# Attention scores over all 128 rows, with the keys of each head laid between zeros

## The chip, the cores and the metric

One core of a Trainium2 chip runs the whole program. The time is the device time of one execution in microseconds. The engines are TensorE (PE; PEld is its weight load), VectorE (DVE), ScalarE (ACT), GpSimd (POOL) and the queue that starts most DMAs (SP).

## The reference

Two layers of a decoder over 256 tokens of width 1024. Each layer has a mixer with two groups of eight heads of 64 columns and then a feed-forward part: a dense SwiGLU in the first layer, the best two of eight experts in the second. Cut to what matters here:

```
u = rmsnorm(h); proj = u @ w_in                       # queries, keys, values of both groups
A: s = q_norm . k_norm * SCALE + bias[dist]           # two key branches (selected, window),
   o = softmax(masked s) @ v                          #   4 query heads share one key head;
                                                      #   and a branch over 15 compressed keys
B: the same with a key and a value head per query head, dilated masks
h = h + [rmsnorm(o_a), rmsnorm(o_b)] @ w_out          # then the feed-forward part
```

With 256 tokens the top-k selection of blocks covers every block, so both branches of group A are dense causal attention.

## The kernel before

All products are matrix products over blocks of 128 tokens (t = 0, 1), with the projections in a two-part form: `product3` (L406) multiplies high and low parts of both operands in three matmuls, L408, L409 and L410. The projection (tile `pj`, L418), the output product (tile `y`, L754) and the scores of group A use it. The weights come in pieces of 1 MB through SP (L74) and are split into their parts by ScalarE (L92) and VectorE (L93).

`attention` first projects group A's keys and values, then its queries, and calls `group_a` (L676) while the projections of group B (`B_CHUNKS`) are still to be done. `heads_t` (L496) turns normalised queries and keys with transposes (tile `ht`, L504), so that the 64 columns of a head lie on 64 of the 128 partitions: two heads share a tile, one on the partitions 0 to 63, the other on 64 to 127. For group A the copies from PSUM are `split_psum` (L340: ScalarE L346 writes the high part, VectorE L347 the low), for group B one ScalarE copy (L509). Queries of group A lie in `qta`, keys in `kta`; group B has both in `qktb`.

`branch` (L511) works through units of heads: the `scores` function fills a PSUM bank (tile `sc`), VectorE adds the bias table and takes the row minimum (L523, tile `ns`), ScalarE takes the exponential with its row sum (L525), four transposes turn the unit's 512 columns (tile `pT`, L532), VectorE or ScalarE copies them (tile `pt`, L537 or L535), and a product with the values follows (tile `o`, L544). Group A has four units for t = 0, with 4 x 128 columns, and eight for t = 1, with 2 x 256; group B two and four. In `scores` a slice `p` of 64 partitions is chosen on both operands:

```
p = slice(g * 64, g * 64 + 64)                                   # group A, L701
product3(..., qh[p, qi, c], ql[p, qi, c], kh[p, :, 0:J], kl[p, :, 0:J], True, True)
```

so each of these matmuls contracts over 64 rows of the array. All others of the stage contract over 128; those of the compression (`hid`, `kvc`) write 32 columns of the array.

The instructions of each engine are put in a fixed order when the program is built, by a scheduler that spreads the matmuls of the next projection, and in group B those of the output product of group A, between the steps of `branch`. An engine goes through its order and waits where an operand is not there yet. Tiles with a tag share memory: `qta` has the tag x2, `qktb` x4, and a new tile with a tag waits for the last reader of the old one. PSUM banks with the tag tr (two) serve the scores, the transposes and several others; group B may use the bank cmp too.

Of the kernel before, what the change touches and what calls it, by code (L numbers as in the profile page):

```python
# [10 lines left out]
F32 = mybir.dt.float32  # L11
F32R = mybir.dt.float32r
# [3 lines left out]
AF = mybir.ActivationFunctionType  # L16
# [5 lines left out]
S = 256  # L22
# [119 lines left out]
def trunk_kernel(ctx: ExitStack, tc: tile.TileContext, T: dict, out: bass.AP):  # L142
    nc = tc.nc
    pe, act, dve, pool, sp = nc.tensor, nc.scalar, nc.vector, nc.gpsimd, nc.sync

    const = ctx.enter_context(tc.tile_pool(name="const", bufs=1))
    main = ctx.enter_context(tc.tile_pool(name="main", bufs=1))
# [9 lines left out]
    def tr_bank(name):  # L157
        return bank("tr", TR, name)
# [23 lines left out]
    for l in range(L):  # L182
# [25 lines left out]
        else:  # L208
            seq = [(e, c) for e in range(NE) for c in range(len(MOE_CHUNKS))]
            first = len(specs)  # L210
            for i in range(len(seq) + 1):
                if i < len(seq):
                    e, c = seq[i]
# [126 lines left out]
    def split_psum(hi, lo, src, scale=None):  # L340

        if scale is None:
            act.activation(hi, src, AF.Copy)
            dve.tensor_tensor(out=lo, in0=src, in1=hi.bitcast(F32), op=ALU.subtract)
        else:
            act.activation(hi, src, AF.Copy, scale=scale)  # L346
            dve.scalar_tensor_tensor(out=lo, in0=src, scalar=scale, in1=hi.bitcast(F32),  # L347
                                     op0=ALU.mult, op1=ALU.subtract)
# [57 lines left out]
    def product3(dst, xh, xl, wh, wl, first, last):  # L406

        pe.matmul(dst, xh, wh, start=first, stop=False)  # L408
        pe.matmul(dst, xl, wh, start=False, stop=False)  # L409
        pe.matmul(dst, xh, wl, start=False, stop=last)  # L410
# [10 lines left out]
    def attention(l, apool, hi, lo, following):  # L421
# [21 lines left out]
        pa = main.tile([128, NT, W_A - 512], F32, name="pa", tag="x6")  # L443
        pb = main.tile([128, NT, 1024], F32, name="pb", tag="x5")
# [48 lines left out]
                    dve.tensor_tensor(out=v, in0=v, in1=r[:, t, 2 * i:2 * i + 2].unsqueeze(2)  # L493
                                      .to_broadcast([128, 2, HD]), op=ALU.mult)

        def heads_t(dst, pj, c0, n, scale):  # L496

            for i in range(0, n, 2):
                m = min(2, n - i)
                b = tr_bank("ht")  # L500
                for j in range(m):
                    for t in range(NT):
                        c = c0 + (i + j) * 128
                        pe.transpose(b[:, j * S + t * 128:j * S + (t + 1) * 128], pj[:, t, c:c + 128], ident)  # L504
                if isinstance(dst, tuple):
                    hi, lo = [d[:, i:i + m, :].rearrange("p i t -> p (i t)") for d in dst]
                    split_psum(hi, lo, b[:, :m * S], scale)
                else:
                    act.activation(dst[:, i:i + m, :].rearrange("p i t -> p (i t)"), b[:, :m * S], AF.Copy, scale=scale)  # L509

        def branch(units, t, scores, vpj, tbl, banks):  # L511

# [162 lines left out]

        def group_a(dq):  # L676
            q = main.tile([128, 2, 4, S], F32R, name="qta", tag="x2")
            k = apool.tile([128, 2, 2, S], F32R, name="kta")
            qh, ql, kh, kl = q[:, 0], q[:, 1], k[:, 0], k[:, 1]
            norm_heads(dq, qa, 0, "qa", paired=True)  # L680
            norm_keys()
            heads_t((qh, ql), qa, 0, 4, qg[:, l:l + 1])
            heads_t((kh[:, 0:1], kl[:, 0:1]), pa, 256, 1, hg[:, 3 + l * 3:4 + l * 3])
            heads_t((kh[:, 1:2], kl[:, 1:2]), pa, 512, 1, hg[:, 4 + l * 3:5 + l * 3])
            if COMPRESS_FIRST:
                bd, kct = compress(kv)

            e3 = apool.tile([128, NT, 24], F32, name="e3")
            act.activation(e3, pa[:, :, 768:792], AF.Exp, scale=-1.0)
            dve.tensor_scalar(out=e3, in0=e3, scalar1=1.0, scalar2=None, op0=ALU.add)  # L690
            dve.reciprocal(out=g3.rearrange("p t i b -> p t (i b)"), in_=e3)

            for t in range(NT):
                J = 128 * (t + 1)
                o = [acc_bank(f"o{br}") for br in range(2)]
                den = [apool.tile([128, 8], F32, name=f"den{br}", tag="den", bufs=4) for br in range(2)]

                def scores(b, u):
                    for i in range(0, len(u), 2):
                        g, qi = divmod(u[i][0], 4)  # L700
                        p = slice(g * 64, g * 64 + 64)  # L701
                        c = slice(t * 128, (t + 1) * 128)
                        product3(b[:, i * J:(i + 2) * J].rearrange("p (b j) -> p b j", b=2), qh[p, qi, c], ql[p, qi, c],
                                 kh[p, :, 0:J], kl[p, :, 0:J], True, True)

                n = 2 // (t + 1)
                units = [[(g * 4 + u * n + i, (384, 640)[br] + g * HD, o[br], den[br])
                          for i in range(n) for br in range(2)] for u in range(4 // n) for g in range(2)]
                branch(units, t, scores, pa, ta, BANKS_A)
                for br in range(2):  # L710
                    combine(o[br], den[br], t, br + 1)
            if not COMPRESS_FIRST:
                bd, kct = compress(kv)
            for t in range(NT):
                compressed(t, qh, ql, kct, bd)

        def group_b(ob):
            qkt = main.tile([128, 8, S], F32, name="qktb", tag="x4")
            qt, kt = qkt[:, 0:4], qkt[:, 4:8]
            heads_t(kt, pb, 512, 4, hg[:, 10 + l:11 + l])  # L720
            heads_t(qt, pb, 0, 4, qg[:, 8 + l:9 + l])
            for t in range(NT):
                J = 128 * (t + 1)
                n = 4 // (t + 1)
                o = acc_bank("o")
                den = apool.tile([128, 8], F32, name="den", tag="den", bufs=4)

                def scores(b, u):
                    for i, (hd, _, _, _) in enumerate(u):
                        qi, r = divmod(hd, 2)  # L730
                        p = slice(r * 64, r * 64 + 64)
                        pe.matmul(b[:, i * J:(i + 1) * J], qt[p, qi, t * 128:(t + 1) * 128], kt[p, qi, 0:J],
                                  start=True, stop=True)

                units = [[(2 * (u * n + i) + r, (2 * (u * n + i) + r) * HD, o, den) for i in range(n)]
                         for u in range(4 // n) for r in range(2)]
                branch(units, t, scores, vb, (tb[:, 0:4], tb[:, 4:8]), BANKS_B)
                rd = apool.tile([128, 8], F32, name="rd", tag="rd", bufs=2)
                dve.reciprocal(out=rd, in_=den)
                dve.tensor_tensor(out=ob[:, t, :].rearrange("p (i d) -> p i d", d=HD),  # L740
                                  in0=o.rearrange("p (i d) -> p i d", d=HD),
                                  in1=rd.unsqueeze(2).to_broadcast([128, 8, HD]), op=ALU.mult)
# [454 lines left out]
    hi, lo = parts()  # L1197
    for c in range(2):
        lift(R_AN, 0, c * 512, 512, hi, lo)
    hg, qg, relb, w2, wr = late_constants()  # L1200
    for l in range(L):
# [23 lines left out]
        if l % 2 == 0:  # L1225
            hi, lo = ffn(l, *nxt)
# [59 lines left out]
```

## Time and profile before

| | |
|---|---|
| median of three runs | 1484.54 us (1482.44 to 1486.54) |
| profiled execution | 1485.44 us, its span 1483.3 us |
| TensorE busy | 1444.2 us, 97% |
| VectorE busy | 1188.5 us, 80% |
| ScalarE busy | 982.4 us, 66% |
| group A, first and second layer | about 56 to 114 us and 400 to 458 us of the span |
| group B, first and second layer | about 136 to 161 us and 479 to 506 us |
| feed-forward of the second layer | from about 540 us to the end |

The stages overlap, since projections and output products run between the steps of the attention; the limits in the table are those between which most of a stage's own instructions lie. In the rows further down a line on busy time gives, behind a stretch and its length, the busy us of PE, PEld, DVE, ACT and POOL, each with its number of instructions in brackets. A timeline line gives start, duration, engine, line, operation, tiles, and in square brackets the idle time before it with what ended it. A record of TensorE runs from the start of a matmul to its modelled end, and records of matmuls that follow one another overlap.

### The profile page before, as it was taken

Reading aid. Unit: us, or ns where it says so; the run is one execution under the profiler, and the core shown is the slowest. Engines: PE = TensorE matmul, PEld = TensorE weight load, DVE = VectorE, ACT = ScalarE, POOL = GpSimd, SP = SyncE. Lnnn points to the kernel's source line nnn. Section 1 sums busy time; section 2 is a strip of 40 time slices with the busy share of each in tenths; the row PEclk is TensorE's granted clock in tenths of the full one; section 3 lists DMA queues with packets and bytes.
Section 4 is the critical chain, followed back from the end, with each engine's and each line's share of the span. In section 5 each row is a group of like instructions: output and inputs, shape, how many; then the busy total and the mean of one; then the engine's idle time right before and its main releaser. Section 6 shows DMA issues by size and latency. Waiting matters only on the chain.

```text
span 1483.3 us, 19457 instructions
## 1 busy us (share of the span) xinstructions
PE 1444.2 (97%) x7166; PEld 1168.7 (79%) x7166; DVE 1188.5 (80%) x1391; ACT 982.4 (66%) x1005; POOL 7.9 (1%) x17
## 2 busy tenths in 40 slices
PE   7999999999999979999999999999999999999997
PEld 6777888888877868877878878888888888888886
DVE  4566855555667669999999999889999888888885
ACT  5455654444555458887887787678787677667773
POOL 2000000000000000000000000000000000000000
PEclk9999999999999979999999999999999999999999
DMA  8822355556734459999999999999999999999990
GB/s 266 289 83 86 128 187 196 193 192 205 229 115 158 141 200 353 393 392 395 394 393 394 394 393 393 394 385 390 395 394 393 389 360 367 328 341 355 366 354 31
DMA packets 201063, 437.72 MB, mean 295 GB/s; under 512 B 9464, under 2 KB 26096, under 8 KB 200944
## 3 DMA queue, kind: packets, MB, share of 16 engines
q1 hardware_dynamic: 198304, 435.16, 80.7%
q8 instruction: 81, 1.33, 0.4%
q10 hardware_dynamic: 2176, 0.52, 0.2%
q0 software_dynamic: 464, 0.40, 0.1%
q14 instruction: 38, 0.31, 0.1%
HBM read 434.45 MB, written 1.08 MB: 294 GB/s over the span
## 4 chain that ended last, share of the span: by engine, by line
PE 86%; DMA 7%; DVE 3%; ACT 1%; issue 1%; SPq 0%; DVEq 0%; ACTq 0%
DMA raw<-in_exp_w_up_dram 7%; PE eg L408 6%; PE eg L409 6%; PE eg L410 6%; PE ey L409 3%; PE ey L410 3%; PE ey L408 3%; PE eu L410 3%; PE eu L409 3%; PE eu L408 3%; PE pj L410 3%; PE pj L408 3%; PE pj L409 3%; PE ey L977 2%; PE y L410 2%; PE y L409 2%
## 5 line engine op out<-in xcount | busy, mean ns | idle before, releaser
L132 DVE TENSOR_TENSOR wlo<-raw,whi 128x2048 fp32r<-128x2048 f32 x336 | 758.2, 2286 | 57.7 <-PE ey L410 19.0
L125 ACT ACTIVATE whi<-raw 128x2048 fp32r<-128x2048 f32 x336 | 638.8, 1914 | 102.6 <-PE eu L409 26.6
L93 DVE TENSOR_TENSOR wlo<-raw,whi 128x1024 fp32r<-128x1024 f32 (+1 forms) x130 | 154.6, 1193 | 103.5 <-ACT whi L92 100.8
L92 ACT ACTIVATE whi<-raw 128x1024 fp32r<-128x1024 f32 (+1 forms) x130 | 133.5, 1032 | 116.7 <-PE y L409 41.3
L408 PE MATMUL eg<-whi,xe 128*128 128x512 f32 x448 | 182.5, 407 | 0.0
L409 PE MATMUL eg<-whi,xe 128*128 128x512 f32 x448 | 177.8, 397 | 0.0
L410 PE MATMUL eg<-wlo,xe 128*128 128x512 f32 x448 | 177.7, 397 | 0.1
L410 PEld LDWEIGHTS eg<-wlo,xe 128*128 128x128 f32 x448 | 84.7, 189 | 20.8 <-DVE wlo L132 0.5
L409 PEld LDWEIGHTS eg<-whi,xe 128*128 128x128 f32 x448 | 84.8, 189 | 17.9
L408 PEld LDWEIGHTS eg<-whi,xe 128*128 128x128 f32 x448 | 84.7, 189 | 17.8
L977 PE MATMUL ey<-wlo,eth 128*128 128x512 f32 x224 | 89.2, 398 | 3.4 <-DVE wlo L132 2.9
L977 PE MATMUL eu<-wlo,xe 128*128 128x512 f32 x224 | 89.0, 397 | 1.9 <-DVE wlo L132 1.8
L410 PE MATMUL eu<-wlo,xe 128*128 128x512 f32 x224 | 88.7, 396 | 1.2 <-DVE wlo L132 1.2
L976 PE MATMUL eu<-whi,xe 128*128 128x512 f32 x224 | 88.8, 397 | 0.0
L409 PE MATMUL eu<-whi,xe 128*128 128x512 f32 x224 | 88.6, 395 | 0.0
L408 PE MATMUL eu<-whi,xe 128*128 128x512 f32 x224 | 88.6, 395 | 0.0
L408 PE MATMUL ey<-whi,eth 128*128 128x512 f32 x224 | 87.9, 392 | 0.7 <-ACT eth L900 0.7
L976 PE MATMUL ey<-whi,eth 128*128 128x512 f32 x224 | 88.4, 395 | 0.0
L409 PE MATMUL ey<-whi,eth 128*128 128x512 f32 x224 | 87.5, 390 | 0.2 <-DVE eth L903 0.2
L410 PE MATMUL ey<-wlo,eth 128*128 128x512 f32 x224 | 87.5, 391 | 0.0
L900 ACT ACTIVATE eth<-eT 128x512 fp32r<-128x512 f32 x56 | 33.3, 595 | 72.9 <-PE eT L997 50.9
L408 PE MATMUL pj<-whi,uhi 128*128 128x512 f32 (+1 forms) x192 | 75.7, 396 | 0.8 <-ACT qv L453 0.8
(316 smaller groups left out, 2378.5 us busy)
## 6 DMA issues: line engine op xcount, KB each, us to landing
raw<-in_exp_w_gate_dram SPq DMA_DIRECT2D x112, 1024.0 KB, 10.6
raw<-in_exp_w_up_dram SPq DMA_DIRECT2D x112, 1024.0 KB, 11.0
raw<-in_exp_w_down_dram SPq DMA_DIRECT2D x112, 1024.0 KB, 11.3
raw<-in_w_in_dram SPq DMA_DIRECT2D x20, 1024.0 KB, 5.6
raw<-in_ffn_w_gate_dram SPq DMA_DIRECT2D x10, 1024.0 KB, 5.0
raw<-in_ffn_w_up_dram SPq DMA_DIRECT2D x10, 1024.0 KB, 5.0
raw<-in_ffn_w_down_dram SPq DMA_DIRECT2D x10, 1024.0 KB, 5.0
raw<-in_cmp_w_dram SPq DMA_DIRECT2D x8, 1024.0 KB, 5.8
```

Of the source, the lines that this page charges most:

```text
L92: self.nc.scalar.activation(hi, src, AF.Copy)
L93: self.nc.vector.tensor_tensor(out=lo, in0=src, in1=hi.bitcast(F32), op=ALU.subtract)
L125: ws.nc.scalar.activation(hi, src, AF.Copy)
L132: self.ws.nc.vector.tensor_tensor(out=lo, in0=src, in1=hi.bitcast(F32), op=ALU.subtract)
L408: pe.matmul(dst, xh, wh, start=first, stop=False)
L409: pe.matmul(dst, xl, wh, start=False, stop=False)
L410: pe.matmul(dst, xh, wl, start=False, stop=last)
L900: act.activation(x[:, :, 0, :], b.rearrange("p (k t) -> p k t", k=4), AF.Copy)
L976: pe.matmul(b, x[:, k, MIX], wh, start=first, stop=False)
L977: pe.matmul(b, x[:, k, MIX], wl, start=False, stop=last)
```

## The change

The keys get a tile with one copy of the 128 partitions for each half. `kta` grows from [128, 2, 2, S] to [128, 2, 2, 2, S] and group B's keys move from `qktb` into an own tile `ktb` [128, 2, 4, S] with the tag x2; the queries of group B keep x4 as `qtb`. GpSimd fills both key tiles with zeros once per layer. `heads_t` gets a switch `apart`: with it the copy from PSUM is made in two, of 64 partitions each, and each goes to its own half of the tile. So in the copy for one head the other head's 64 rows are zero. `scores` then takes all 128 partitions of the queries and of the chosen copy of the keys. Queries and evacuations without the switch stay as they were.

```
-        def heads_t(dst, pj, c0, n, scale):
+        def heads_t(dst, pj, c0, n, scale, apart=False):
...
-                if isinstance(dst, tuple):
-                    hi, lo = [d[:, i:i + m, :].rearrange("p i t -> p (i t)") for d in dst]
-                    split_psum(hi, lo, b[:, :m * S], scale)
-                else:
-                    act.activation(dst[:, i:i + m, :].rearrange("p i t -> p (i t)"), b[:, :m * S], AF.Copy, scale=scale)
+                for p, r in ((slice(0, 64), 0), (slice(64, 128), 1)) if apart else ((slice(0, 128), None),):
+                    def part(d):
+                        d = d if r is None else d[:, r]
+                        return d[p, i:i + m, :].rearrange("p i t -> p (i t)")
+
+                    if isinstance(dst, tuple):
+                        split_psum(part(dst[0]), part(dst[1]), b[p, :m * S], scale[p])
+                    else:
+                        act.activation(part(dst), b[p, :m * S], AF.Copy, scale=scale[p])
...
-            k = apool.tile([128, 2, 2, S], F32R, name="kta")
+            k = apool.tile([128, 2, 2, 2, S], F32R, name="kta")
+            pool.memset(k.bitcast(F32), 0.0)
...
+            heads_t((kh[:, :, 0:1], kl[:, :, 0:1]), pa, 256, 1, hg[:, 3 + l * 3:4 + l * 3], True)
+            heads_t((kh[:, :, 1:2], kl[:, :, 1:2]), pa, 512, 1, hg[:, 4 + l * 3:5 + l * 3], True)
...
-                        p = slice(g * 64, g * 64 + 64)
-                        product3(b[:, i * J:(i + 2) * J].rearrange("p (b j) -> p b j", b=2), qh[p, qi, c], ql[p, qi, c],
-                                 kh[p, :, 0:J], kl[p, :, 0:J], True, True)
+                        product3(b[:, i * J:(i + 2) * J].rearrange("p (b j) -> p b j", b=2), qh[:, qi, c], ql[:, qi, c],
+                                 kh[:, g, :, 0:J], kl[:, g, :, 0:J], True, True)
...
-            qkt = main.tile([128, 8, S], F32, name="qktb", tag="x4")
-            qt, kt = qkt[:, 0:4], qkt[:, 4:8]
-            heads_t(kt, pb, 512, 4, hg[:, 10 + l:11 + l])
+            qt = main.tile([128, 4, S], F32, name="qtb", tag="x4")
+            kt = main.tile([128, 2, 4, S], F32, name="ktb", tag="x2")
+            pool.memset(kt, 0.0)
+            heads_t(kt, pb, 512, 4, hg[:, 10 + l:11 + l], True)
...
-                        pe.matmul(b[:, i * J:(i + 1) * J], qt[p, qi, t * 128:(t + 1) * 128], kt[p, qi, 0:J],
+                        pe.matmul(b[:, i * J:(i + 1) * J], qt[:, qi, t * 128:(t + 1) * 128], kt[:, r, qi, 0:J],
```

The number of matmuls and their columns stay the same. The scheduler orders them anew. Three places follow; `x2` at the end of a row stands for two such instructions in a row.

TensorE, first layer, group A, one unit of the second half: `pT` are the transposes of this unit, `sc` the scores of the next, `o` the product with the values, `kcT` a step of the compression. Before:

```order
L532 MATMUL pT<-cc,ns 128x128 x2
L408 MATMUL sc<-kta,qta 128x512
L532 MATMUL pT<-cc,ns 128x128 x2
L409 MATMUL sc<-kta,qta 128x512
L410 MATMUL sc<-kta,qta 128x512
L544 MATMUL o_640<-pa,pt 128x64 x2
```

After:

```order
L537 MATMUL pT<-cc,ns 128x128 x2
L408 MATMUL sc<-kta,qta 128x512
L409 MATMUL sc<-kta,qta 128x512
L537 MATMUL pT<-cc,ns 128x128 x2
L410 MATMUL sc<-kta,qta 128x512
L549 MATMUL o_645<-pa,pt 128x64 x2
```

One score has moved from behind the unit's last transposes to ahead of them; one score is left between these and the product with the values.

TensorE, first layer, the end of group B: `ut` are the transposes of group B's output `ob`, `y<-...,po` the output product of group A, `y<-...,pob` that of group B. Before:

```order
L544 MATMUL o<-qv,pt 128x64 x8
L357 MATMUL ut<-cc,ob 128x128 x2
L409 MATMUL y<-whi,po 128x512
L410 MATMUL y<-wlo,po 128x512
L408 MATMUL y<-whi,po 128x512
L357 MATMUL ut<-cc,ob 128x128 x6
L409 MATMUL y<-whi,po 128x512
L410 MATMUL y<-wlo,po 128x512
L408 MATMUL y<-whi,po 128x512
L409 MATMUL y<-whi,po 128x512
L410 MATMUL y<-wlo,po 128x512
L408 MATMUL y<-whi,pob 128x512 x2
```

After:

```order
L549 MATMUL o<-qv,pt 128x64 x4
L357 MATMUL ut<-cc,ob 128x128
L408 MATMUL y<-whi,po 128x512
L409 MATMUL y<-whi,po 128x512
L410 MATMUL y<-wlo,po 128x512
L549 MATMUL o<-qv,pt 128x64 x4
L357 MATMUL ut<-cc,ob 128x128 x7
L408 MATMUL y<-whi,pob 128x512 x2
```

The eight output matmuls of group A behind the last product of group B stand ahead of it now.

ScalarE, first layer, the start of group B. Before:

```order
L346 ACTIVATE po<-ut,gv_141 128x256 x2
L509 ACTIVATE qktb<-ht,hg 128x512 x2
L509 ACTIVATE qktb<-ht,qg 128x512 x2
L525 ACTIVATE ns,den<-ns,mn 128x128 x8
L92 ACTIVATE whi<-raw 128x1024
```

After:

```order
L346 ACTIVATE po<-ut,gv_141 128x256 x2
L514 ACTIVATE ktb<-ht,hg 64x512 x4
L514 ACTIVATE qtb<-ht,qg 128x512 x2
L530 ACTIVATE ns,den<-ns,mn 128x128 x8
L92 ACTIVATE whi<-raw 128x1024
```

The two copies of the keys are four, of 64 partitions each.

## Rows read from the trace of the kernel before

**Rows 1.** Busy time by stretch: stretch, us, engines with instructions, PEclk, DMA share, GB/s.

```profile
56.00:114.00 58.00, 57.91 (x375) 41.46 (x367) 35.85 (x133) 32.60 (x93) 0.00 (x0) 1.00 0.39 133
136.00:160.00 24.00, 23.95 (x146) 17.94 (x145) 13.53 (x52) 14.41 (x43) 0.00 (x0) 1.00 0.21 72
400.00:458.00 58.00, 57.98 (x375) 41.92 (x372) 36.62 (x136) 32.37 (x93) 0.00 (x0) 1.00 0.40 137
540.00:1483.00 943.00, 926.30 (x4292) 754.37 (x4291) 853.85 (x529) 709.63 (x484) 0.00 (x0) 1.00 0.97 363
```

**Rows 2.** Instructions on the score tiles: duration ns min/median/max, first and last start.

```profile
L732 PE MATMUL sc<-qktb x64: 272/374/480, 139.3 to 495.1; 64*128 64x128 f32 x32, 64*128 64x256 f32 x32
...
L408 PE MATMUL sc<-kta,qta x32: 275/439/502, 60.8 to 451.4; 64*128 64x256 f32 x16, 64*128 64x512 f32 x16
```

**Rows 3.** Timeline of TensorE, group A, first layer: start us, duration us, engine, line.

```profile
90.95 0.40 PE L408 MATMUL pj<-whi,uhi 128*128 128x512 f32 x1
90.95 0.19 PEld L409 LDWEIGHTS pj<-whi,ulo 128*128 128x128 f32 x1
91.19 0.40 PE L409 MATMUL pj<-whi,ulo 128*128 128x512 f32 x1
```

**Rows 4.** Timeline, a stretch with four changes of rows, first layer.

```profile
91.88 0.38 PE L532 MATMUL pT<-cc,ns 128*128 128x128 f32 x2
...
92.19 0.49 PE L408 MATMUL sc<-kta,qta 64*128 64x512 f32 x1
...
92.61 0.44 PE L532 MATMUL pT<-cc,ns 128*128 128x128 f32 x2
...
93.32 0.39 PE L410 MATMUL sc<-kta,qta 64*128 64x512 f32 x1
...
93.64 0.50 PE L409 MATMUL pj<-whi,ulo 128*128 128x512 f32 x1
...
93.98 0.40 PE L410 MATMUL pj<-wlo,uhi 128*128 128x512 f32 x1
```

**Rows 5.** Waits in the attention stage of the first layer: us in total, times, longest.

```profile
DVE ns L523 <- PE sc L410: 10.2, 7, 2.1
...
PEld pT L532 <- ACT ns L525: 1.1, 4, 0.3
```

**Rows 6.** Timeline, the links of group A's chain, first layer.

```profile
63.15 0.39 ACT L525 ACTIVATE ns<-ns,mn 128x128 f32<-128x128 f32 x1
...
96.54 0.44 PE L532 MATMUL pT<-cc,ns 128*128 128x128 f32 x2
...
97.24 0.39 PE L410 MATMUL sc<-kta,qta 64*128 64x512 f32 x1
...
97.72 0.97 PEld L544 LDWEIGHTS o<-pa,pt 128*128 128x128 f32 x8 [0.52 <-ACT pt L535]
...
98.93 0.44 PE L532 MATMUL pT<-cc,ns 128*128 128x128 f32 x2
```

**Rows 7.** Instructions on the key tiles.

```profile
L346 ACT ACTIVATE kta<-ht,hg x4: 474/474/475, 59.5 to 403.0; 128x256 fp32r<-128x256 f32 x4
...
L509 ACT ACTIVATE qktb<-ht,hg x4: 680/686/690, 136.9 to 479.2; 128x512 f32<-128x512 f32 x4
```

**Rows 8.** Costliest groups: count, busy us, mean ns of one, idle before and releaser.

```profile
L125 ACT ACTIVATE whi<-raw 128x2048 fp32r<-128x2048 f32 x336 | 638.8, 1914 | 102.6 <-PE eu L409 26.6
L93 DVE TENSOR_TENSOR wlo<-raw,whi 128x1024 fp32r<-128x1024 f32 (+1 forms) x130 | 154.6, 1193 | 103.5 <-ACT whi L92 100.8
```

**Rows 9.** Timeline, the last readers of the queries in group A, first layer.

```profile
121.92 0.53 PE L654 MATMUL cs<-kct,qta 128*128 128x32 f32 x4
```

**Rows 10.** Timeline, group B's first scores, first layer.

```profile
139.26 1.71 PE L732 MATMUL sc<-qktb 64*128 64x128 f32 x16
```

**Rows 11.** Timeline, behind the last product of group B, first layer.

```profile
160.63 0.69 DVE L740 TENSOR_TENSOR ob<-o,rd 128x512 f32<-128x512 f32 x1 [1.98 <-PE o L544]
...
161.37 0.64 PEld L357 LDWEIGHTS ut<-cc,ob 128*128 128x128 f32 x6 [0.29 <-DVE ob L740]
```

More of the change, by code (lines that the diff above doesn't have):

```diff
@@ L682, in group_a @@
             heads_t((qh, ql), qa, 0, 4, qg[:, l:l + 1])
-            heads_t((kh[:, 0:1], kl[:, 0:1]), pa, 256, 1, hg[:, 3 + l * 3:4 + l * 3])
-            heads_t((kh[:, 1:2], kl[:, 1:2]), pa, 512, 1, hg[:, 4 + l * 3:5 + l * 3])
+            heads_t((kh[:, :, 0:1], kl[:, :, 0:1]), pa, 256, 1, hg[:, 3 + l * 3:4 + l * 3], True)
+            heads_t((kh[:, :, 1:2], kl[:, :, 1:2]), pa, 512, 1, hg[:, 4 + l * 3:5 + l * 3], True)
             if COMPRESS_FIRST:
@@ L730, in scores @@
                         qi, r = divmod(hd, 2)
-                        p = slice(r * 64, r * 64 + 64)
-                        pe.matmul(b[:, i * J:(i + 1) * J], qt[p, qi, t * 128:(t + 1) * 128], kt[p, qi, 0:J],
+                        pe.matmul(b[:, i * J:(i + 1) * J], qt[:, qi, t * 128:(t + 1) * 128], kt[:, r, qi, 0:J],
                                   start=True, stop=True)
```

## The prediction

> **What bounds the kernel now.** I read the busy time by stretch first, then TensorE's own timeline inside the attention stage, and last the waits there. By stretch [rows 1] TensorE is busy for 57.91 of 58 us in the first layer's group A, for 23.95 of 24 us in its group B and for 57.98 of 58 in the second layer's group A, with VectorE and ScalarE at 63% and below. The clock is granted in full there, so TensorE runs at 2.4 GHz and the clock gate has no part in this.
>
> "Busy" needs a second look, because a matmul's record includes its fill and drain. So I read the distances from start to start. Two projection matmuls of 512 columns start 0.24 us apart (0.23 for most) although a record lasts 0.40, and the weights of the next are loaded under the running one [rows 3]: that is the undisturbed pace. The score matmuls do not keep it. In the stretch of [rows 4] the array goes from transposes over all 128 rows to scores over 64 rows and back, twice. From the transposes at 91.88 to the projection at 93.98 are 2.10 us. In them stand 4 transposes, 3 scores of 512 columns (the one left out is at 92.98) and 1 projection: 4 x 0.11 + 4 x 0.23 = 1.36 us at the undisturbed pace (a pair of transposes lasts 0.11 longer than one would, 0.38 for 0.27). The other 0.74 us belong to four changes between 64-row and 128-row work, about 0.185 us each. One sees what they consist of: from the score at 93.32 to the projection at 93.64 are 0.32 where 0.23 would do, and that projection's record is 0.50 long instead of 0.40. It starts only when the matmul before has drained, and its own weight load is inside its record.
>
> The waits of the first layer's stage [rows 5] show who follows whom: VectorE waits 10.2 us for group A's scores, while TensorE's loads wait 1.1 us for ScalarE's exponentials. TensorE is late, the others wait for it.
>
> **What the change removes.** The 160 score instructions (64 in group B, and 96 in group A, three lines of 32 each, of which one is shown in [rows 2]) read all 128 rows afterwards, as the transposes, the projections and the products with V already do. In TensorE's order before, they stand in 67 runs between other work, 53 in group A and 14 in group B over both layers. Each run costs an entry and an exit. Of these 134 changes five are against the 32-column matmuls of the compression; the changed order still has 30 changes against those, the old one had 34, so one or two stay. Group A: 106 x 0.185 = 19.6 us. Group B: 28 x 0.185 = 5.2 us. The columns streamed stay the same, so nothing else of TensorE's work shrinks.
>
> Two rules of the Trainium skill bear on this, and one speaks against it. "TensorEngine Tiling (Array Packing)", Key Properties, says that a change of tiling mode drains TensorE: the drain at 93.64 agrees with it. "TensorE: Matmul & The Clock Gate", Part 3, says that a weight load overlaps a running matmul only if their row groups differ; by it every score over the full array would expose its load, and some 3 us of the sum below would be left. The trace disagrees: full-array loads lie under full-array matmuls in [rows 3].
>
> **What it adds.** *Concurrency lost.* The first scores of group B use the two row halves in turn and partly run at once: 16 instructions end after 1.71 us [rows 10], where 16 at 0.11 and a fill would take about 2.0. I charge 0.3 us per layer, 0.6 in all.
>
> *Evacuations in halves.* In the rows an evacuation's time goes by its columns (0.474 us for 256, 0.686 for 512 [rows 7]), and only the partitions are halved here. So ScalarE's 4 copies of group A's keys become 8 of the same length, their 4 counterparts on VectorE too, and the 4 copies of group B's keys become 8. Per layer that is 0.95 us on ScalarE ahead of group A's first score, about as much on VectorE, and 1.37 us on ScalarE ahead of group B's. Queued behind them are the exponentials on ScalarE and, in TensorE's order, the scores and all that follows them. The cover is the projection, compression and output matmuls that the order puts ahead of the first scores: four more of the output projection in group B. If it were gone, all is exposed: 2 x (0.95 + 1.37) = 4.6 us; the other end is nothing. I take 0.3 us per layer in group A and 0.4 in group B, nearer to the covered end because the covering matmuls stand in the order.
>
> *Zeros on GpSimd.* Four fills of 128x2048. The trace has no such fill; GpSimd is idle in the stage [rows 1], so from below they cost nothing. The nearest row of this shape is ScalarE's 128x2048 copy at 1.914 us [rows 8], and I take 2 us. Group A's fill waits for nothing in the first layer, and in the second for the end of the first layer's attention, long before. Group B's can start when the last compressed scores have read the queries (121.92 and 0.53 us [rows 9]) and is needed at the first key copy at 136.9 [rows 7]: 14 us of room. It costs nothing up to seven times my value, and one for one beyond, in each layer.
>
> *What is late next.* A faster TensorE meets waits that the changes of mode used to cover. In group A's second half the chain has two links. From the start of a unit's last score (97.24) over VectorE and half of ScalarE's work to the first transpose (98.93 [rows 6]) are 1.7 us, in which some 1.4 us of other work must lie behind the score's 0.23. The product with V is 8 x 0.11 = 0.9, so two projections more are enough; a unit that has none or one there loses 0.2 to 0.5. From the last transposes (96.54, the second 0.11 later) to the product with V (97.72) are 1.1 us, at whose end TensorE already waits 0.52 for the copy. After the change the order often leaves two scores and one or two projections there, 0.7 to 1.0 us, and in the unit shown above a single score of 0.23. I add 0.1 to 0.3 for most units and 0.7 for that one: with the first link 1.3 us per layer. In the first half a unit needs four exponentials of 0.39 us, one for each transpose [rows 6], and the order leaves less than that between the transposes; some 0.5 us are short on two or three units of four, another 1.3 us per layer. For the weight splits of 1.2 us on VectorE [rows 8] that will now and then stand in front of a score's reduction I take 0.8 us per layer. With the 0.3 of the evacuations: 3.7 us per layer, 7.4 in all. The bounds: nothing if every unit finds cover, and all 19.6 us if the chain through VectorE and ScalarE were the limit; their shares in [rows 1] put it nearer to the small end.
>
> In group B the eight output matmuls that used to follow the last product with V (sixteen in the second layer) are spent earlier, as the second piece of the order shows. Before, VectorE's copy (160.63, 0.69 us) was covered by them except for 0.29 us ahead of the transposes at 161.37 [rows 11]. Now TensorE waits there: 1.0 us per layer. With 0.4 for the evacuations and 0.4 for short links as in group A, group B loses 1.8 us per layer, 3.6 in all, besides the 0.6 of concurrency.
>
> **The sum.** Group A 19.6 - 7.4 = 12.2. Group B 5.2 - 0.6 - 3.6 = 1.0. Together 13.2; I say 13.5, because a single matmul between two runs pays more than the mean. What follows attention hangs on its end: the weight loads of both feed-forward parts wait for buffers that it frees, and in the last 943 us TensorE is busy for 926 [rows 1], so the shift should arrive whole. The profiled execution took 1485.44 us (its span 1483.3), 0.9 above the median of the runs. 1485.44 - 13.5 = 1471.9, and on the median's scale **1471.0 us**.
>
> **The rivals.** *All is kept.* The waits that I added vanish in the idle time that VectorE and ScalarE have [rows 1, 5]: 19.6 + 5.2 - 0.6 = 24.2, less 1 for evacuations, so about 1461. Against it stands the thin unit in the order.
>
> *The chain takes it.* If the loop of scores, VectorE, exponentials, transposes, copy and product is the true pace and the drains only filled its gaps, TensorE's gain turns into waits and the time stays: 1481 to 1488. For it: the 0.52 us wait at 97.72. Against it: the 10.2 us that VectorE waits for scores.
>
> *Slower, by the halved evacuations.* Place: ScalarE ahead of the first scores of both groups. Price: 4.6 us, with the bare tail of group B 6.6, so 1491. It decides the sign if the drains were covered to three quarters, so that under 6.6 us of the 24.8 come free. For it: 134 changes of which none was seen alone. Against it: TensorE's 99% in group A.
>
> *It doesn't do what it says.* If weight loads over the full array lay exposed at every score: 67 of the 160 pay for a load already, so 93 x 0.11 = 10 us come on top of my forecast, 1481. [Rows 3] speak against it. This is what the Trainium skill's Part 3 of "TensorE: Matmul & The Clock Gate" would give.
>
> **How the numbers follow.** Forecast (1464 to 1477): 0.60. All is kept (below 1464): 0.14. Little kept (1477 to 1480): 0.11. No change, by the chain or by exposed loads: 0.09. Slower: 0.06. A measurement of this kernel tells 0.3%, some 4.5 us, from no change; so faster takes 0.60 + 0.14 + 0.11 = 0.85, the same 0.09 and slower 0.06. The range for 8 in 10 goes from 1462 to 1481: half of the second case lies below it (0.07), and most of the last two above it (0.12).
>
> **What will show it.** Scores of 128*128 that start 0.11 or 0.23 us after their neighbours, with the load under the matmul before, show the removal right. Group A's stretch should shrink from 58 to about 52 us per layer, group B's hardly. Waits for the copies at the product with V, and a gap behind group B's last product, show the new waits. A fill longer than 14 us, or 0.50 us records still at each run, would make the forecast wrong.

## The result, and the profile after

The changed kernel takes 1468.17 us (median of six runs, 1465.25 to 1469.78), the kernel before 1485.26 in the same set (1482.44 to 1488.31). The ratio is 0.9884 with an interval of 0.9869 to 0.9898: 17.1 us faster, 3.6 more than the 13.5 forecast, and inside the range. The profiled execution took 1466.53 us, its span 1464.7.

To see where the time went I cut both traces at the same instructions. Group A's stage runs from the first transpose of its queries to the start of its last product with V; group B's from its first transpose to the first output matmul of its own half.

| us | before | after | difference |
|---|---|---|---|
| program up to group A, first layer | 55.19 | 52.33 | -2.86 |
| group A, first layer | 61.25 | 53.60 | -7.65 |
| between A and B, first layer | 19.79 | 19.78 | -0.01 |
| group B, first layer | 27.01 | 26.85 | -0.16 |
| up to group A, second layer | 235.30 | 235.35 | +0.05 |
| group A, second layer | 59.65 | 53.09 | -6.56 |
| between A and B, second layer | 19.81 | 19.79 | -0.02 |
| group B, second layer | 27.51 | 26.85 | -0.66 |
| from there to the end | 977.79 | 977.09 | -0.70 |

Group A gives 14.2 us and group B 0.8, together 15.0. I don't count the first row to the change: among the kernels below it lies between 51.8 and 55.6 us, in no order with their edits.

The busy time by stretch, first layer (group A, then B), then second layer; the columns are those of [rows 1]:

```profile
52.33:105.93 53.60, 52.72 (x405) 43.44 (x403) 39.78 (x148) 34.20 (x96) 0.00 (x0) 1.00 0.50 171
125.70:152.60 26.90, 25.76 (x165) 20.99 (x165) 17.28 (x57) 18.79 (x51) 0.07 (x1) 1.00 0.24 78
387.90:441.00 53.10, 52.42 (x395) 43.25 (x395) 39.35 (x145) 34.26 (x96) 0.00 (x0) 1.00 0.45 152
460.80:487.70 26.90, 25.77 (x165) 20.98 (x165) 16.43 (x57) 17.75 (x50) 0.00 (x0) 1.00 0.47 153
```

TensorE now has idle time, 0.9 and 0.7 us in group A and 1.1 in each group B, where the same stages of the kernel before have at most 0.1. The clock is granted in full, as before.

The scores in the list of instructions by tile, against [rows 2]: the shape is 128*128 and the median record of group A's line L408 falls from 439 to 380 ns.

```profile
L737 PE MATMUL sc<-ktb,qtb x64: 275/363/435, 130.1 to 479.6; 128*128 128x128 f32 x32, 128*128 128x256 f32 x32
...
L408 PE MATMUL sc<-kta,qta x32: 276/380/483, 59.0 to 433.3; 128*128 128x256 f32 x16, 128*128 128x512 f32 x16
```

TensorE's timeline in group A, a unit with the same instructions as the stretch of [rows 4]:

```profile
84.00 0.38 PE L537 MATMUL pT<-cc,ns 128*128 128x128 f32 x2
84.14 0.48 PE L408 MATMUL sc<-kta,qta 128*128 128x512 f32 x1
84.45 0.38 PE L537 MATMUL pT<-cc,ns 128*128 128x128 f32 x2
84.59 0.48 PE L409 MATMUL sc<-kta,qta 128*128 128x512 f32 x1
84.90 0.39 PE L410 MATMUL sc<-kta,qta 128*128 128x512 f32 x1
85.13 0.39 PE L408 MATMUL pj<-whi,uhi 128*128 128x512 f32 x1
85.36 0.39 PE L409 MATMUL pj<-whi,ulo 128*128 128x512 f32 x1
```

From the first transposes to the second projection are 85.36 - 84.00 = 1.36 us, which is 4 x 0.11 + 4 x 0.23, the undisturbed pace. The same instructions took 2.10 in [rows 4]. The score at 84.90 and the projections behind it follow one another by 0.23 with records of 0.39, so no load stands open between these full-array matmuls. The Trainium skill, "TensorE: Matmul & The Clock Gate", Part 3, has a load overlap only where row groups differ; the measurement is against it here.

The waits in group A, first layer (us in total, times, longest), then the second layer:

```profile
DVE ns L528 <- PE sc L410: 4.0, 4, 1.4
...
PEld o L549 <- ACT pt L540: 1.1, 2, 0.8
...
PEld pT L537 <- ACT ns L530: 0.8, 2, 0.6
...
PEld o L549 <- DVE pt L542: 0.4, 2, 0.3
```

```profile
DVE ns L528 <- PE sc L410: 3.2, 4, 1.3
...
PEld pT L537 <- ACT ns L530: 1.1, 2, 0.7
...
PEld o L549 <- ACT pt L540: 1.0, 4, 0.3
...
PEld o L549 <- DVE pt L542: 0.7, 3, 0.3
```

The same two kinds of waits of TensorE's loads in the kernel before, first layer:

```profile
PEld o L544 <- ACT pt L535: 0.5, 1, 0.5
...
PEld pT L532 <- ACT ns L525: 0.2, 1, 0.2
```

VectorE waits 4.0 us for scores where it waited 10.2 [rows 5]; TensorE's loads wait 2.3 us in the first layer and 2.8 in the second for exponentials and copies, where they waited 0.7 and 0.4. TensorE has become a little the waiting side. The thin unit of the order is one of the places:

```profile
87.25 0.44 PE L537 MATMUL pT<-cc,ns 128*128 128x128 f32 x2 [0.43 <-ACT ns L530]
...
88.14 0.48 PE L410 MATMUL sc<-kta,qta 128*128 128x512 f32 x1
89.07 1.10 PE L549 MATMUL o<-pa,pt 128*128 128x64 f32 x8 [0.45 <-ACT pt L540]
```

### The profile page after: what moved, and what is told of

The parts are those of the page before. It is cut to its first block, busy times and chain, and to the rows that moved or that the text cites. A ratio compares the mean times of both kernels' runs of the same rounds, so it can differ in the third digit from the quotient of the medians.

```text
span 1464.7 us, 19495 instructions
## 1 busy us (share of the span) xinstructions
PE 1422.1 (97%) x7166; PEld 1165.2 (80%) x7166; DVE 1190.8 (81%) x1395; ACT 986.8 (67%) x1013; POOL 15.2 (1%) x21
## 4 chain that ended last, share of the span: by engine, by line
PE 85%; DMA 9%; DVE 3%; ACT 2%; issue 1%; SPq 0%; DVEq 0%; ACTq 0%
DMA raw<-in_exp_w_up_dram 7%; PE eg L408 6%; PE eg L410 6%; PE eg L409 6%; PE ey L409 3%; PE ey L410 3%; PE ey L408 3%; PE eu L410 3%; PE eu L409 3%; PE eu L408 3%; PE pj L410 3%; PE pj L408 3%; PE pj L409 3%; PE y L408 2%; PE ey L982 2%; PE eu L981 2%
## 5 line engine op out<-in xcount | busy, mean ns | idle before, releaser
L408 PE MATMUL eg<-whi,xe 128*128 128x512 f32 x448 | 181.8, 406 | 0.0
L409 PEld LDWEIGHTS eg<-whi,xe 128*128 128x128 f32 x448 | 84.4, 188 | 17.8
L408 PEld LDWEIGHTS eg<-whi,xe 128*128 128x128 f32 x448 | 84.4, 188 | 17.6
L408 PE MATMUL eu<-whi,xe 128*128 128x512 f32 x224 | 88.6, 395 | 0.0
L408 PE MATMUL ey<-whi,eth 128*128 128x512 f32 x224 | 87.9, 392 | 0.7 <-ACT eth L905 0.7
L408 PE MATMUL pj<-whi,uhi 128*128 128x512 f32 (+1 forms) x192 | 74.7, 391 | 1.6 <-ACT qv L453 1.6
## 6 DMA issues: line engine op xcount, KB each, us to landing
raw<-in_exp_w_gate_dram SPq DMA_DIRECT2D x112, 1024.0 KB, 11.1
```

## The experiments

All numbers of stages are cut as in the table above. Ratios are to the kernel before, run beside each on the same chip.

### The changed kernel once more

> The changed kernel once more, beside the runs of the kernel before on this chip. By the stages of the profiles the change takes 15.0 us (14.2 in group A, 0.8 in group B); the first timing gave 17.2 us with an interval of 15 to 19.5. Theory (the change gains nothing outside the attention, and what stands beyond 15 us is the start of the program, which differs from run to run): a ratio of 0.989 to 0.991 and the stages of group A and B again within 0.1 us; the start of group A's query transposes falls anywhere between 51 and 56 us. Rival (the start gains too): they start near 52 us again.

No edit. Measured: 1469.19 us, ratio 0.9909 (0.9891 to 0.9927), so 13.7 us faster, with stages of 53.59, 26.86, 53.06 and 26.86 us. The stages repeat to 0.05 us. The medians of two sets of the same pair differ by 3.4 us in their gain, 17.1 and 13.7, so I take the gain from the stages: 15.0. The rest of the first set's 17.1 is outside the changed stages.

### Group A alone, and group B alone

Group A as after and group B as before:

```
-            qt = main.tile([128, 4, S], F32, name="qtb", tag="x4")
-            kt = main.tile([128, 2, 4, S], F32, name="ktb", tag="x2")
-            pool.memset(kt, 0.0)
-            heads_t(kt, pb, 512, 4, hg[:, 10 + l:11 + l], True)
+            qkt = main.tile([128, 8, S], F32, name="qktb", tag="x4")
+            qt, kt = qkt[:, 0:4], qkt[:, 4:8]
+            heads_t(kt, pb, 512, 4, hg[:, 10 + l:11 + l])
...
-                        pe.matmul(... qt[:, qi, t * 128:(t + 1) * 128], kt[:, r, qi, 0:J],
+                        pe.matmul(... qt[p, qi, t * 128:(t + 1) * 128], kt[p, qi, 0:J],
```

> Group A as after the change, group B as before it. Theory (each change of rows costs 0.185 us, and group B gives back nearly all that it gains): 14 to 15 us faster than before, about 1470.5, within 2 us of the changed kernel. Rival (both groups gain by their share of the 134 changes, 4 to 1): 17 x 0.8 = 13.5 us faster, and 3.5 us slower than the changed kernel. Rival (the start of the program, 2.9 us earlier in the changed kernel's profile, belongs to the change): the first transposes of group A's queries start at 52 us here too, otherwise anywhere between 52 and 55.

Measured: 1469.11 us, ratio 0.9907 (0.9887 to 0.9927). Group A's stages are 53.59 and 53.00 us, group B's 27.02 and 27.03. The reverse, group A as before and group B as after:

```
-            k = apool.tile([128, 2, 2, 2, S], F32R, name="kta")
-            pool.memset(k.bitcast(F32), 0.0)
+            k = apool.tile([128, 2, 2, S], F32R, name="kta")
...
-                        product3(... qh[:, qi, c], ql[:, qi, c], kh[:, g, :, 0:J], kl[:, g, :, 0:J], True, True)
+                        product3(... qh[p, qi, c], ql[p, qi, c], kh[p, :, 0:J], kl[p, :, 0:J], True, True)
```

> Group B as after the change, group A as before it. Theory: 28 changes x 0.185 = 5.2 us gained, and given back by the lost concurrency (0.6), the doubled key copies on ScalarE and the bare end of the group (3.6): 0 to 1.5 us faster than before, not to be told from it. Rival (group B gains by its share of the changes): 3.5 to 5 us faster, about 1481.

Measured: 1483.65 us, ratio 1.0001 (0.9988 to 1.0015), stages 61.25 and 59.70, 26.86 and 27.58. The gain is group A's. In group B 0.5 us of the second layer come from the order that group A's change sets (27.51 to 27.03 with B as it was). Its own part is worth 0.2 us per layer beside the new group A; beside the old one it is 0.15 in the first layer, and the second is 0.07 longer.

### The new layout with scores over 64 rows

Keys apart, copies in halves, zeros and the order of all instructions as in the changed kernel; the scores read the 64 rows of their head. This takes back only the contraction.

```
+                        p = slice(g * 64, g * 64 + 64)
...
-                        product3(... qh[:, qi, c], ql[:, qi, c], kh[:, g, :, 0:J], kl[:, g, :, 0:J], True, True)
+                        product3(... qh[p, qi, c], ql[p, qi, c], kh[p, g, :, 0:J], kl[p, g, :, 0:J], True, True)
...
+                        p = slice(r * 64, r * 64 + 64)
-                        pe.matmul(... qt[:, qi, t * 128:(t + 1) * 128], kt[:, r, qi, 0:J],
+                        pe.matmul(... qt[p, qi, t * 128:(t + 1) * 128], kt[p, r, qi, 0:J],
```

> The changed kernel with its zeros, its halved copies and its order of instructions on every engine, which is the same word for word; only the scores read the 64 rows of their head again. Theory (the rows make the difference): 61 runs of scores, 122 changes x 0.185 = 22.6 us, of which 3 to 7 us lie in waits that the changed kernel has anyway: 1483 to 1488, about the time of the kernel before. Rival (the new order of instructions brought the gain): within 3 us of the changed kernel, below 1472.

Measured: 1489.63 us, ratio 1.0053 (1.0035 to 1.0072). The order and the layout by themselves gain nothing in the time; that rival falls. My figure was 1.6 us too low at its upper end. The kernel is even some 7 us slower than the one before. By the stages of the profiles its group B is 1.7 and 1.2 us longer, and the first layer of its group A lost about 5 us to the clock, as is shown below; but for that its group A is 1 us shorter in all. The same unit as above, on TensorE:

```profile
88.41 0.38 PE L537 MATMUL pT<-cc,ns 128*128 128x128 f32 x2
88.72 0.49 PE L408 MATMUL sc<-kta,qta 64*128 64x512 f32 x1
89.14 0.44 PE L537 MATMUL pT<-cc,ns 128*128 128x128 f32 x2
89.51 0.50 PE L409 MATMUL sc<-kta,qta 64*128 64x512 f32 x1
89.85 0.39 PE L410 MATMUL sc<-kta,qta 64*128 64x512 f32 x1
90.17 0.50 PE L408 MATMUL pj<-whi,uhi 128*128 128x512 f32 x1
90.50 0.39 PE L409 MATMUL pj<-whi,ulo 128*128 128x512 f32 x1
```

2.09 us for 1.36, in the same order: 0.73 for four changes, 0.18 each. That is the direct price in this unit. The stages against those of the changed kernel are 11.1 and 7.2 us longer in group A and 1.84 and 1.86 in group B. Group A has 46 changes in the first layer and 48 in the second. Why do the two differ by 4 us? The busy time by stretch of group A, first and second layer, and three stretches of the first, has the answer in the number behind POOL, the granted clock:

```profile
53.06:117.78 64.72, 64.03 (x406) 47.00 (x403) 40.37 (x148) 34.38 (x96) 0.00 (x0) 0.92 0.41 141
...
401.58:461.87 60.29, 59.62 (x395) 43.84 (x395) 39.83 (x145) 34.48 (x96) 0.00 (x0) 1.00 0.39 134
```

```profile
88.00:92.00 4.00, 3.97 (x21) 2.63 (x19) 1.90 (x10) 0.83 (x2) 0.00 (x0) 1.00 0.00 0
92.00:96.00 4.00, 3.34 (x15) 2.33 (x15) 3.52 (x22) 2.53 (x9) 0.00 (x0) 0.86 0.00 0
96.00:100.00 4.00, 4.00 (x11) 2.07 (x11) 1.74 (x4) 0.54 (x2) 0.00 (x0) 0.50 0.00 0
```

In the first layer the clock fell to 1.2 GHz near 94.9 us (it is 0.93 from 94 to 95, then 0.50) and came back near 105. The projections show it: they follow one another by 0.43 us there, by 0.23 elsewhere. With a mean of 0.92 over 64.72 us, 0.08 x 64.72 = 5.2 us of clock are missing, and without them the stage would be about 59.5, 5.9 longer than after. (This is an estimate; it holds if all of the stretch goes at the array's pace, and the clock's two digits leave 0.3 us open in it, here and below.) So in group A the full contraction is worth 6 to 7 us per layer, 0.13 to 0.15 per change, where the direct price in the unit is 0.18. The second layer tells where the difference lies. Both kernels have there the same 395 TensorE instructions in the same order, so that their distances from start to start can be compared one by one. At the changes and right behind them those of this kernel are longer by 7.9 us in all: 0.165 for a change in the mean of 48, with units that pay less than the one shown. At products with V and ahead of transposes they are shorter by 0.7 us, which makes 7.2: these are waits of the changed kernel that the slower order covers. In that layer its loads wait 1.7 us for copies ahead of products with V, those of this kernel 0.2.

The waits of its first layer show the drain in another way:

```profile
PEld pT L537 <- issue: 3.0, 10, 0.7
...
PEld sc L408 <- issue: 1.7, 8, 0.3
...
PEld pj L408 <- issue: 1.4, 4, 0.4
```

Weight loads that wait for nothing but "issue", ahead of transposes, scores and projections. In part this layer ran at the lower clock; the second one, at the full clock, has 2.2, 1.8 and 0.9 us in these three lines. In the changed kernel each such line ahead of scores and projections has 0.2 us, and there is none ahead of transposes.

### Only the middle one of three

Of the three matmuls of a score in group A the middle one reads 64 rows. If a change is what costs, this pays two changes for each of 32 matmuls; if each 64-row matmul costs by itself, a third.

```
-                        product3(... qh[:, qi, c], ql[:, qi, c], kh[:, g, :, 0:J], kl[:, g, :, 0:J], True, True)
+                        pe.matmul(d, qh[:, qi, c], kh[:, g, :, 0:J], start=True, stop=False)
+                        pe.matmul(d, ql[p, qi, c], kh[p, g, :, 0:J], start=False, stop=False)
+                        pe.matmul(d, qh[:, qi, c], kl[:, g, :, 0:J], start=False, stop=True)
```

> The changed kernel in the same order of instructions; in group A only the middle one of the three matmuls of each score (32 of 96) reads the 64 rows of its head. Theory (the cost is per change): each of the 32 stands between matmuls over 128 rows, so 64 changes x 0.185 = 11.8 us, less 1 to 3 us that fall into waits: 9 to 11 us slower than the changed kernel, about 1478. Rival (a matmul over 64 rows is itself the slow one): 32 of the 160 score instructions, so a fifth of the whole difference, 3.4 us, about 1471.5.

Measured: 1478.50 us, ratio 0.9972 (0.9958 to 0.9986), 9.3 us above the changed kernel by 1469.19 and 1478.50. The rival with a price per matmul gave 3.4. Its group A:

```profile
52.47:114.61 62.14, 61.26 (x405) 46.95 (x403) 40.19 (x148) 34.35 (x96) 0.00 (x0) 0.95 0.43 146
...
396.59:454.99 58.40, 57.69 (x396) 44.43 (x395) 39.63 (x145) 34.34 (x96) 0.00 (x0) 1.00 0.42 139
```

The second layer is 5.3 us longer than after, 0.166 for each of its 32 changes, with the clock in full. The first is 8.5 longer, of which 0.05 x 62.14 = 3.1 is clock: 5.4, the same. So 32 of the 96 matmuls cost 10.7 us where all 96 cost 5.9 + 7.2 = 13.1: the price goes by changes (64 against 94), not by matmuls.

### One layer at a time

To separate the changes' price from the clock, the same edit as in the layout experiment, in one layer only.

```
+                        p = slice(g * 64, g * 64 + 64) if l == 1 else slice(0, 128)
...
+                        p = slice(r * 64, r * 64 + 64) if l == 1 else slice(0, 128)
```

> The changed kernel, with the scores of the second layer alone contracted over the 64 rows of their head; layout, copies and the order of all instructions are those of the changed kernel, so that 47 runs in group A and 14 in group B get back their... two changes less the pairs that touch 32-column work: 61 changes in all. Theory now: a change costs TensorE 0.15 to 0.17 us in group A, as the second layer of the kernel with all scores over 64 rows showed (7.2 us over 47 changes, clock granted in full), and 1.9 us in all in group B. Then group A's stage of the second layer is 7.2 us longer than in the changed kernel (about 60.3), group B's 1.9 (about 28.7), the granted clock stays 1.00 there, and the median is 9 us above the changed kernel's, about 1477.5. Rival: a change costs 0.2 us and more, as the first layer of that kernel gave (11.1 us over 47): the stage is 11 us longer and the median 13 us above, 1481.

Measured: 1478.35 us, ratio 0.9970 (0.9951 to 0.9988), 9.2 above the changed kernel's 1469.19. The median is near the theory's 1477.5. The profiled execution, of 1480.70, is not: group A's second layer took 63.31 us, and this time the clock fell there, where I had expected 1.00.

```profile
388.35:451.66 63.31, 62.64 (x396) 45.90 (x395) 39.87 (x145) 34.47 (x96) 0.00 (x0) 0.95 0.38 128
```

The surplus over the changed kernel is 10.2; less 0.05 x 63.31 = 3.2 of clock it is 7.0. Group B took 1.9 more. The first layer alone (the same edit with `l == 0`):

> The changed kernel, with the scores of the first layer alone contracted over 64 rows, everything else as in the changed kernel. In the kernel with all scores over 64 rows the granted clock was halved from about 94.5 to 105 us of the first layer, behind two waits around a product with V. Theory: the changes cost the same 7.2 + 1.9 us here as in the second layer, and what the first layer shows beyond is the clock alone: group A's stage is 11.1 us longer than in the changed kernel with a granted clock of 0.92 in it, 3.9 us of that for the clock, and the median is 13 us above, about 1481.5. If the clock does not fall this time, the stage is 7.2 us longer and the median 9 us above. Rival: the first layer's changes are dearer whatever the clock: 11 us with a clock of 1.00.

Measured: 1480.92 us, ratio 0.9970 (0.9959 to 0.9981).

```profile
53.92:115.66 61.74, 61.05 (x405) 44.94 (x403) 38.91 (x142) 34.27 (x96) 0.00 (x0) 0.97 0.42 142
```

8.1 us more in group A, of which 0.03 x 61.74 = 1.9 is clock: 6.3. The fall was shorter than in the layout experiment, from 98 to 102 us, so the stage was 3 us under the forecast. The rival of dearer changes in the first layer falls: wherever the clock is taken out, 5.9 to 7.2 us are left, in either layer.

### Half of group B's key copies on VectorE

```
+                    elif r:
+                        dve.tensor_scalar(out=part(dst), in0=b[p, :m * S], scalar1=scale[p], scalar2=None, op0=ALU.mult)
```

> The changed kernel, but of group B's keys VectorE copies the half of the partitions 64 to 127, beside ScalarE with the other half, so that ScalarE does four copies ahead of the first scores again and not six. Theory (ScalarE's doubled copies delay group B by 0.4 us per layer as forecast): group B's stage falls from 26.85 to about 26.4 us in both layers, group A stays; 1 us in the whole, hardly to be told in the time. Rival (the copies are wholly covered by the output matmuls ahead of the scores): 26.85 us again. Rival (they are exposed at the full price of 1.37 us): 25.5 us.

Measured: 1468.44 us, ratio 0.9899 (0.9881 to 0.9917), not to be told from the changed kernel by its time. Group B's stages are 26.52 and 26.54 us instead of 26.86: 0.33 per layer come back when half of the copies leave ScalarE, close to the 0.4 that I had charged for all of their delay. What they cost on VectorE is not in it. It is the one version tried that is shorter than the changed kernel in its stages, by 0.6 us in all, which the time doesn't resolve.

### Another bank for group A's scores and transposes

Can a third PSUM bank take the waits out of group A's chain? It is the compression's.

```
-    BANKS_A = (tr_bank,)
+    BANKS_A = (tr_bank, cmp_bank)
```

> The changed kernel with a third PSUM bank for group A's scores, the one of the compression, as group B has it; the order of instructions in group A changes with it. Theory (what group A still loses, some 2.5 us per layer, are waits in the chain of scores, VectorE, ScalarE, transposes and copy, and not TensorE's work): scores that can run ahead shorten them, group A's stages fall by 1 to 3 us per layer, 1463 to 1467. Rival (the compression, which needs that bank step by step, is held up and its matmuls come late): group A gets longer by 1 to 4 us per layer.

Measured: 1500.34 us, ratio 1.0111 (1.0093 to 1.013), 31 us slower than the changed kernel. Group A's stage is 41.5 us instead of 53.6, but the stretch behind it, up to group B, 46.9 instead of 19.8; together 15.0 more in the first layer and 16.8 in the second. The rival was right in its mechanism, and its size was far too small. The two stretches of the first layer:

```profile
53.30:94.80 41.50, 38.13 (x231) 30.01 (x232) 27.07 (x121) 22.33 (x77) 0.00 (x0) 0.96 0.08 26
94.80:141.60 46.80, 39.78 (x291) 32.08 (x291) 32.59 (x85) 20.97 (x36) 1.81 (x1) 0.93 0.60 211
```

and the compression in it, on TensorE:

```profile
97.05 5.24 PE L606 MATMUL hid<-raw,xp 128*32 128x128 f32 x128 [1.96 <-issue]
...
105.05 0.38 PE L630 MATMUL kvc<-w,gelu 128*32 128x64 f32 x4 [2.01 <-issue]
```

The compression's 128 matmuls, all but four of which the changed kernel has between 51.3 and 62.7 us as cover in the chain, stand in one piece behind group A, and its chain of short steps lies bare. Group A has lost its cover too: TensorE is idle for 3.4 us of its 41.5. The clock is 0.96 and 0.93, so part of the loss is the clock's.

## Why the prediction held, point by point

The mechanism held, and the number came out close partly by luck: in group A two terms of the sum were too large and worked against one another, and half of group B's gain has another source than its terms. The first set's 17.1 us has 2 that no changed stage shows; the second set's 13.7 has none.

**The pace and the price of a change.** Right for the unit that it was read from, and seen directly: with nothing but the rows different, the unit takes 2.09 or 1.36 us, 0.18 for each change (0.185 forecast). Too high as the price of all changes: over a stage it is 0.165 in the mean, by the second layer of the layout experiment and by the middle-one experiment. One reading went further than the trace: I wrote that the projection at 93.64 [rows 4] starts only when the matmul before has drained, but that record's modelled end is 93.32 + 0.39 = 93.71. What the trace shows is that the start is late and that the weight load starts with it. A recount of the order gives 54 runs in group A and 13 in group B for my 53 and 14; the sum is the same.

**Group A, 19.6 - 7.4 = 12.2.** Measured 14.2. Both terms were too large. At 0.165 each the old order's 108 changes were worth about 17.8 us and not 19.6 (an estimate, since it carries the mean of the new order over to the old one). Then 17.8 - 14.2 = 3.6 us came back, not 7.4. Loads ahead of the product with V and of the transposes wait 5.1 us in both layers together, 4.0 more than before the change, which fits by size. By place I was half right: some 4 us of them stand in the units of the second half, for which I had forecast 2.6, and about 1 in the first half, for which I had forecast 2.6 too. The thin unit lost the 0.7 that I had given it: from its score at 88.14 to the product with V at 89.07 are 0.93 us where 0.23 would do (the 0.45 in brackets counts from the record's modelled end). The halved copies of group A, for which I had 0.3 per layer, are in the 3.6 us too, and no run shows them alone. That the rest is these waits is argued from size and place; no experiment took them away, since the one that tried (the third bank) moved the compression instead.

**Group B, 5.2 - 0.6 - 3.6 = 1.0.** Measured 0.8, and it is luck that they agree: 0.5 of it is the order that group A's change sets, and group B's own part is 0.35 at most. Four of its terms can be read. The full contraction is worth 3.7 us in the new order (1.84 and 1.86), where 5.2 - 0.6 = 4.6 stood. The concurrency was as forecast: the first sixteen scores take

```profile
130.09 2.02 PE L737 MATMUL sc<-ktb,qtb 128*128 128x128 f32 x16
```

2.02 us against 1.71 [rows 10]. The copies in halves cost about 0.33 per layer (0.4 forecast). The bare end, against [rows 11]:

```profile
150.71 0.69 DVE L745 TENSOR_TENSOR ob<-o,rd 128x512 f32<-128x512 f32 x1
...
151.46 0.87 PE L357 MATMUL ut<-cc,ob 128*128 128x128 f32 x6 [0.67 <-DVE ob L745]
...
152.57 0.96 PE L408 MATMUL y<-whi,pob 128*128 128x512 f32 x4 [0.24 <-ACT pob L346]
```

TensorE waits 0.67 us for VectorE's copy and 0.24 for ScalarE's, 0.9 where I had 1.0. With that 3.7 - 0.7 - 1.8 = 1.2 us should be left; the 0.9 between this and its own part would be the short links, for which I had 0.8, but no run shows them alone.

**The fills and the copies.** As forecast. The lists of the two key tiles:

```profile
L725 POOL MEMSET ktb<- x2: 1808/1812/1815, 112.0 to 447.1; 128x2048 f32 x2
...
L514 ACT ACTIVATE ktb<-ht,hg x8: 682/684/684, 126.4 to 463.6; 64x512 f32<-64x512 f32 x8
```

```profile
L684 POOL MEMSET kta<- x2: 1824/1828/1833, 10.2 to 152.5; 128x2048 f32 x2
...
L346 ACT ACTIVATE kta<-ht,hg x8: 469/470/472, 56.7 to 393.7; 64x256 fp32r<-64x256 f32 x8
```

A fill takes 1.81 to 1.83 us (2 estimated) and group B's is done 126.4 - 113.8 = 12.6 us before the first key copy. A copy of 64 partitions takes as long as one of 128: 470 ns for 474, 684 for 686 [rows 7].

**What follows shifts whole.** Yes: the stretch up to the second layer moved by 0.05 us and the one to the end by 0.70.

**The rivals.** "All is kept" and "the chain takes it" both have a part of the truth, 14.2 of some 17.8 us in group A kept and 3.6 taken. "Slower, by the halved evacuations" falls by the time, and group B's copies gave 0.33 us per layer where that rival had 1.37; group A's part was not measured alone. Exposed loads fall by the unit at 84.00.

## What to carry to other kernels

Where matmuls of 64 rows stand one by one among matmuls of 128, read the distance from start to start against the pace of the engine, not the busy time, which was 96 to 100% in these stages before and after; each change cost 0.18 us in a dense unit and 0.165 in the mean. Filling the idle rows with zeros removes it if some idle engine can write the zeros early. Not all of the direct price arrives (here 14.2 of some 17.8 us): waits that the drains had covered come out, and the new order shows where, above all at the product with the least work ahead of it.

## What the runs showed that I had not expected

The clock can fall inside the dense stage. In the experiments with 64-row scores the granted clock dropped from 2.4 to 1.2 GHz in group A, for 3 to 10 us, at no fixed place: in the first layer of the layout experiment near 94.9 us, of the middle-one near 94 and of the first-layer one near 98, and in the second layer of the second-layer one. Ahead of it, in the layout experiment, TensorE had waited twice around a product with V:

```profile
92.40 0.44 PE L537 MATMUL pT<-cc,ns 128*128 128x128 f32 x2 [0.43 <-ACT ns L530]
...
94.55 1.72 PE L549 MATMUL o<-pa,pt 128*128 128x64 f32 x8 [0.27 <-ACT pt L540]
```

The changed kernel has the same two waits in the same unit, of 0.43 and 0.45 us, and kept its clock in both profiles, and so did the kernel before. Counted over all profiles but the third bank's, by layer, the new order with 64-row scores lost its clock in group A in four of six, and with scores over all rows in none of ten; the old order with 64-row scores kept it in all four. Scores over all rows don't protect it in general: the clock fell in the third bank's run too, where TensorE is idle for 3.4 of 41.5 us. What decides stays open. The falls mean that a stage time read from one profile must be read beside its granted clock: without that the first layer's 11.1 us would have passed for a price of 0.24 us per change.
